# Products with zeros ahead of two output steps of a state space model, and pooling groups in reverse order on GpSimd

## The chip, the core and the metric

The kernel runs on one core of a Trainium2 chip. A core has five engines, each with its own queue of instructions, which it works off in order: TensorE (PE: matrix products, and PEld, its weight loads), VectorE (DVE), ScalarE (ACT), GpSimd (POOL) and SyncE (SP), which issues most of the DMAs. Engines wait for each other by semaphores. The metric is the device time of one execution in microseconds (us).

## The reference

Two transformer stacks over one sequence of 256 tokens of 1024 channels, in fp32. The first has two layers: a gated delta rule mixer with a SwiGLU feed-forward layer, then a state space mixer (S5) with a mixture of eight experts, of which each token uses two. The second stack has one layer: a mixer and an MLP. The change touches the S5 mixer and the second stack's mixer. What they compute, cut to what matters:

```python
def s5_mixer(x, w_in, lam_re, lam_im, log_dt, b_re, b_im, c_re, c_im, d_skip, w_glu):
    u = (x @ w_in).astype(f32)
    ...
    def step(h, u_c):
        bu = jnp.einsum('gpc,btgc->btgp', b_bar, u_c.astype(jnp.complex64))
        _, hs = lax.associative_scan(binop, (jnp.broadcast_to(a_bar, bu.shape), bu), axis=1)
        hs = hs + a_pow[None] * h[:, None]
        y = jnp.einsum('gcp,btgp->btgc', c, hs).real
        return hs[:, -1], y
    ...
    hid = jax.nn.gelu(y.astype(x.dtype), approximate=False)
    val, gate = jnp.split(hid @ w_glu, 2, axis=-1)
    return val * jax.nn.sigmoid(gate)

def pool_mixer(u, w_pool, pool_scale):
    # four groups of 128 channels, windows 2, 4, 8, 16
    ...
        outs.append(mean - u32[:, :, sl])
    mixed = jnp.einsum('btgc,gcd->btgd', pooled, w_pool)
    return mixed.reshape(B, T, POOL_WIDTH) * pool_scale
```

Beside `pool_mixer`, the second stack's mixer has attention of 8 heads over a 64-column grid of tokens: scores, softmax with a mask, and the product with v.

## The kernel before

Everything runs on one core, one stage after the other, in the order of the reference. Matrix products of fp32 are split: each operand has an upper part (`wh`, `hid[0]`) and a remainder (`wl`, `hid[1]`), and the helper `mm3` issues three products per tile, lines 354, 355 and 356: upper by upper, remainder of the weights by upper, upper by remainder. It keeps the product that it issued last in `self.mm`. Weights come by DMA into `wr` (three buffers); ACT makes `wh` of it (line 308) and DVE, seldom POOL, `wl` (line 310), with five buffers each.

Work beside the main stream is written as generators, which `spawn` puts on a list with a lag; `tick` lets them go on between the products of the main stream. The order on each engine is fixed when the program is built, by a scheduler that knows what each instruction depends on. `tc.issue_after(inst)` makes what is issued inside come behind `inst` in that order; it adds no data.

The helper `warm(n)` (lines 272 to 279) issues n bf16 products of a zero tile of 128 x 64 with 512 zero columns into a PSUM bank of its own that nobody reads. Before the change it is called at four places, with the counts of the table `WARM` (line 45).

**S5** works on eight blocks k of 8 groups of channels. For each k, `maps` builds the matrices of the recurrence (products pbt and pk), `states` turns u (pt), makes the inputs of the states (px), scans on DVE (line 1327) and writes the states at the chunk starts into CC (DVE, line 1337), and `outputs(k)` does the following: eight small products pyi of CC with C (line 1349), a copy Y (ACT, line 1350), products yp of u with a band matrix (line 1358) and of Y with the identity (line 1360), the update of uT (DVE, line 1362), Gelu into h (ACT, line 1364), and the split into hid (ACT line 348, DVE line 349). Twelve products `po` of hid with w_glu per block, lines 354 to 356, follow as soon as hid(k) is there; we call them po(k). While the first blocks run, the last products pu of u = x @ w_in are still being issued. The rest of the w_glu products come behind po(7), one dense stream.

**The second mixer** issues products pqk for q and k (lines 354 to 356), for each pair of heads j the scores (line 1929, psc), the bias (DVE, line 1932), the maximum (lines 1936, 1937), Exp on ACT with the row sums in z (line 1939), the reciprocal of z on DVE (line 1940), and the scaling Pr on POOL (line 1942). z has two buffers. At the same time `pool(g)` runs for the four groups g: g+1 additions w on POOL (line 1976, each with the doubled step of the one before), the product with the reciprocal counts, d (line 1984), the difference d - u (line 1985), and then one product ppl with w_pool (line 1988), a copy m1 on ACT (line 1990) and m2 on DVE (line 1991). pool(g) is spawned in the order g = 0, 1, 2, 3 with the lags 3 to 6.

Of the kernel before, what the change touches and what calls it, by code (L numbers as in the profile page):

```python
# [23 lines left out]
KT = D // 128  # L24
# [17 lines left out]
LAG = dict(nb=6, d=5, dp=4, n=1, rk=3, ks=4, kp=4, inv=7, i0=3, iy=8, i1=2, i2=1, lv=4, rq=4, qs=8, qp=2, v=2)  # L42
S5L = dict(per=4, s0=3, t0=9, m=1, o=0, mb=2, a=2, b=2, c=2, d=4, e=2, f=1, g=1, ct=4, gt=4, keep=2)
MO = dict(d=3, t=2, b=5, a=2, sc=1)
WARM = dict(a=12, b=9, c=20, e=5, f=0)
PACE = (1200, 650)
MAGIC = 12582912.0
CH = 4
NJ = T // CH
# [155 lines left out]
class Kern:  # L205
# [66 lines left out]
    def warm(self, n):  # L272

        if not n:
            return
        pb = self.bank("warm")[:64].rearrange("p (a b) -> p a b", a=8)
        for _ in range(n):
            self.nc.tensor.matmul(pb, lhsT=self.zero, rhs=self.zero[:, None, :].to_broadcast([128, 8, 64]), start=True,
                                  stop=True)


# [111 lines left out]
    def load_first(self):  # L393
# [8 lines left out]
        nc.vector.memset(self.zero, 0.0)  # L402
        self.warm(WARM["a"])
        nc.sync.dma_start(xT[:, 0:4, :], a["xT"][:, 0:1024])
# [842 lines left out]
    def s5(self, tables):  # L1247
        nc, tc, a = self.nc, self.tc, self.a
# [6 lines left out]
        MM, TR = nc.tensor.matmul, nc.tensor.transpose  # L1255
# [84 lines left out]
        def outputs(k):  # L1340

            while k not in known:
                yield 1
            C = B[:, k].rearrange("p g c n -> p (g c n)").rearrange("p (g o c) -> p g (o c)", g=8, o=CH)
            H = CC[:, 8 * k:8 * k + 8, :]
            Y = P2.tile([NJ, CH, 8, 16], F32, tag="Y", name="Y")
            py = self.bank("pyi").rearrange("p (g f) -> p g f", g=8)
            for g in range(8):
                MM(py[:NJ, g, :], lhsT=H[:, g, :], rhs=C[:, g, :], start=True, stop=True)
            nc.scalar.activation(Y.rearrange("j o g c -> j g o c"), py[:NJ].rearrange("p g (o c) -> p g o c", o=CH), AF.Copy)  # L1350
            yield S5L["g"]
            while not hid:
                yield 1
            BD = bds.pop(k)
            yp = self.bank("yp")[:, :T].rearrange("p (o j) -> p o j", o=CH)
            for n in range(CH):
                o = min(n, CH - 2)
                MM(yp[:, o:, :], lhsT=BD[:, n, :], rhs=uT[:, k, 1 + o - n:CH + 1 - n, :], start=n == 0, stop=False)
            for o in range(CH):
                MM(yp[:, o, :], lhsT=Y[:, o].rearrange("j g c -> j (g c)"), rhs=ident[:NJ, :NJ], start=False, stop=o == CH - 1)  # L1360
            y = uT[:, k, 1:, :]
            STT(y, y, self.small("sd", k), yp, op0=ALU.mult, op1=ALU.add)
            h = P2.tile([128, T], F32, tag="h", name="h")
            nc.scalar.activation(h.rearrange("p (j o) -> p o j", o=CH), y, AF.Gelu)
            self.split(hid[0][:, k, :], hid[1][:, k, :], h)
            known.add(("hid", k))
# [17 lines left out]
        def flow():  # L1384
            for s in range(12 * KT):
                due = []
                for f, at in ((outputs, S5L["s0"] + S5L["o"] + S5L["a"] + S5L["b"] + S5L["c"] + S5L["d"]), (states, S5L["s0"]),
                              (maps, S5L["s0"] + S5L["m"])):
                    k, r = divmod(s - at, S5L["per"])
                    if 0 <= k < KT and not r and (k > 1 or f != maps):  # L1390
                        self.spawn(f(k))
                yield 1
# [25 lines left out]
        def done(t, n, po):  # L1418
# [18 lines left out]
            else:  # L1437
                self.warm(WARM["e"])
                for _ in logits(t, n):
# [10 lines left out]
        def logits(t, n):  # L1450

            if n == 0:
                xf[t] = (tables, P)[t].tile([128, KT, 128], F32, tag=("CX", "CY")[t], name="xf")
            if (t, n) == (0, 0):
                pl.append(self.bank("pl"))
            nc.scalar.activation(xf[t][:, 2 * n:2 * n + 2, :], self.turn4(self.rr[:, t, n * 256:n * 256 + 256], 2), AF.Copy)
            yield 1
            for kt in range(2 * n, 2 * n + 2):
                MM(pl[0][32 * t:32 * t + 8, :128], lhsT=self.wr[:, kt, :], rhs=xf[t][:, kt, :], start=kt == 0, stop=kt == KT - 1)

        def routed(t):
# [8 lines left out]
            if t:  # L1470
                with tc.issue_after(turned.ins):
                    self.warm(WARM["b"])
            self.ln_apply(t, self.route(t, pb) if t else None)
# [63 lines left out]
    def moe(self):  # L1537
# [13 lines left out]
        def select(es):  # L1551
            m = es.stop - es.start
            for t in range(2):
                r = TT(Sel[:, t, es], iota[:, None, :].to_broadcast([128, m, 128]),
                       pos[:, t, es].unsqueeze(2).to_broadcast([128, m, 128]), op=ALU.is_equal)
            return r
        chosen = select(slice(0, 2))
        self.warm(WARM["f"])

# [159 lines left out]
        with tc.issue_after(self.mm.ins):  # L1719
            self.warm(WARM["c"])  # L1720
        xn = P.tile([128, 2, D], F32, tag="SelT", name="xn")
# [177 lines left out]
    def mixer(self):  # L1899
        nc, tc, a = self.nc, self.tc, self.a  # L1900
# [5 lines left out]
        MM, TR = nc.tensor.matmul, nc.tensor.transpose  # L1906
# [8 lines left out]
        k = P.tile([128, 4, T], F32, name="k")  # L1915
# [51 lines left out]
        def pool(g):  # L1967

            e = slice(8, 8 + T)
            prev = u[:, g, :]  # L1970
            for i in range(g + 1):
                w = P2.tile([128, T + 16], F32, tag="w", name="w")
                lo, hi = (1, 0) if i == 0 else (2 ** (i - 1), 2 ** (i - 1))
                n = T + 16 - lo - hi if i < g else T
                o = lo if i < g else 8
                PT_(w[:, o:o + n], prev[:, o - lo:o - lo + n], prev[:, o + hi:o + hi + n], op=ALU.add)  # L1976
                if i < g:

                    nc.gpsimd.memset(w[:, 0:o], 0.0)
                    if hi:  # L1980
                        nc.gpsimd.memset(w[:, o + n:], 0.0)
                prev = w
            d = P2.tile([128, T], F32, tag="d", name="d")
            PT_(d, prev[:, e], c2[:, g, :], op=ALU.mult)
            PT_(d, d, u[:, g, e], op=ALU.subtract)
            yield 4
            pb = self.bank("ppl")[:, :T]
            MM(pb, lhsT=wpool[:, g, :], rhs=d, start=True, stop=True)
            sc = self.small("pscale", g)
            nc.scalar.activation(self.m1[:, g, :], pb, AF.Copy, scale=sc)  # L1990
            STT(self.m2[:, g, :], pb, sc, self.m1[:, g, :], op0=ALU.mult, op1=ALU.subtract)
# [12 lines left out]
        pb = self.bank("prr")[:, :T]  # L2004
# [3 lines left out]
        for t in range(2):  # L2008
            self.spawn(first(t, self.pbs[t]))
        for g in range(4):  # L2010
            self.spawn(pool(g), 3 + g)
        for j in range(4):
            for dst in (q, k):
                pb = self.bank("pqk", True)[:, :T]
# [41 lines left out]
```

## Time and profile before

| | us |
|---|---|
| median of 3 runs | 1281.87 (1281.63 to 1282.15) |
| the profiled execution | 1283.42 |
| its span, first to last instruction | 1281.6 |
| PE busy | 1232.8 (96%) |
| DVE busy | 1025.7 (80%) |
| ACT busy | 738.4 (58%) |
| POOL busy | 152.6 (12%) |

The granted TensorE clock has a mean of 0.981 of full speed. The profile comes from one execution, and its times are microseconds from the span's first instruction. A timeline gives an instruction's start, its duration, its engine, line and operation, what it writes and reads, and how many stand in the row; in brackets how long the engine was idle before it, and who ended that. The duration of products that follow each other overlaps with the next one's, so the distance of two starts is what one takes up. The eight small fp32 products of a pyi show as x16.

### The profile page before, as it was taken

How to read it: one execution, taken by the hardware profiler on the slowest of the kernel's cores; microseconds unless marked ns; L12 is line 12 of the kernel's file. 1: busy time of each engine (PE TensorE's matmuls, PEld its weight loads, DVE VectorE, ACT ScalarE, POOL GpSimd, SP SyncE). 2: the span in 40 equal slices, each digit the busy share in tenths (PEclk: the TensorE clock that was granted, in tenths of full speed). 3: DMA queues.
4: the chain of work that ended last, by engine and by line, in shares of the span. 5: the costliest groups of instructions: out<-in, count | busy, mean ns of one | idle time of the engine just before them, and what ended most of it. 6: DMA issues, size and time to landing. Idle time of an engine off the chain costs nothing. (4 is left out here: it accounts for less than half of the span.)

```text
span 1281.6 us, 19707 instructions
## 1 busy us (share of the span) xinstructions
PE 1232.8 (96%) x7579; PEld 1064.4 (83%) x7579; DVE 1025.7 (80%) x1565; ACT 738.4 (58%) x1111; POOL 152.6 (12%) x154
## 2 busy tenths in 40 slices
PE   8999999999998899989999999999999999999997
PEld 7998987999986787758888888888877677999886
DVE  6678878989987788678998999999879785766453
ACT  5744455564433553458777776767767465655442
POOL 2323000000102266110000000000002090000000
PEclk8999999999998999989999999999999899999999
DMA  8344225545794300337998989989977543545551
GB/s 330 128 144 141 88 79 203 179 165 197 209 245 187 131 34 34 132 123 281 359 347 303 352 328 362 339 318 379 341 286 298 197 173 132 198 171 192 193 185 50
DMA packets 45589, 273.37 MB, mean 213 GB/s; under 512 B 9008, under 2 KB 9408, under 8 KB 18096
## 3 DMA queue, kind: packets, MB, share of 16 engines
q1 hardware_dynamic: 40320, 257.12, 54.9%
q10 hardware_dynamic: 4336, 10.19, 2.2%
q0 software_dynamic: 832, 4.73, 1.6%
q8 instruction: 62, 1.02, 0.3%
q14 instruction: 39, 0.32, 0.1%
HBM read 266.51 MB, written 1.31 MB: 209 GB/s over the span
## 5 line engine op out<-in xcount | busy, mean ns | idle before, releaser
L310 DVE TENSOR_TENSOR wl<-wr,wh 128x1024 fp32r<-128x1024 f32 (+1 forms) x380 | 447.5, 1195 | 130.8 <-ACT wh L308 127.8
L308 ACT ACTIVATE wh<-wr 128x1024 fp32r<-128x1024 f32 (+2 forms) x390 | 390.9, 1025 | 241.4 <-PE po L356 79.4
L356 PE MATMUL pup<-wh,xg 128*128 128x512 f32 (+1 forms) x384 | 145.1, 378 | 3.0 <-PEq L1680 3.0
L355 PE MATMUL pup<-wl,xg 128*128 128x512 f32 (+1 forms) x384 | 146.3, 381 | 0.1
L354 PE MATMUL pup<-wh,xg 128*128 128x512 f32 (+1 forms) x384 | 146.3, 381 | 0.0
L310 DVE TENSOR_TENSOR wl<-wx,wh 128x1024 fp32r<-128x1024 f32 (+2 forms) x111 | 124.2, 1152 | 11.2 <-ACT wh L308 9.1
L308 ACT ACTIVATE wh<-wx 128x1024 fp32r<-128x1024 f32 (+1 forms) x112 | 105.0, 981 | 9.9 <-PE pup L356 5.9
L354 PE MATMUL p<-x,wh 128*128 128x256 f32 x320 | 90.7, 284 | 0.3 <-ACT s L1013 0.3
L356 PE MATMUL p<-x,wl 128*128 128x256 f32 x320 | 90.6, 283 | 0.0
L355 PE MATMUL p<-x,wh 128*128 128x256 f32 x320 | 90.5, 283 | 0.0
L356 PEld LDWEIGHTS pup<-wh,xg 128*128 128x128 f32 x384 | 72.6, 189 | 14.3 <-issue 3.4
L355 PEld LDWEIGHTS pup<-wl,xg 128*128 128x128 f32 x384 | 72.7, 189 | 13.8 <-DVE wl L310 3.5
L354 PEld LDWEIGHTS pup<-wh,xg 128*128 128x128 f32 x384 | 72.7, 189 | 10.9 <-issue 0.2
L355 PE MATMUL pdn<-wl,eh 128*128 128x512 f32 x176 | 70.0, 398 | 0.8 <-DVE wl L310 0.8
L354 PE MATMUL pdn<-wh,eh 128*128 128x512 f32 x176 | 69.9, 397 | 0.0
L356 PE MATMUL pdn<-wh,eh 128*128 128x512 f32 x176 | 69.5, 395 | 0.0
L354 PE MATMUL pm<-x,wh 128*128 128x256 f32 x224 | 63.5, 283 | 0.0
L356 PE MATMUL pm<-x,wl 128*128 128x256 f32 x224 | 63.4, 283 | 0.0
L355 PE MATMUL pm<-x,wh 128*128 128x256 f32 x224 | 63.4, 283 | 0.0
L354 PEld LDWEIGHTS p<-x,wh 128*128 128x128 f32 x320 | 61.4, 192 | 0.6 <-ACT s L1013 0.5
L355 PEld LDWEIGHTS p<-x,wh 128*128 128x128 f32 x320 | 61.4, 192 | 0.1
L356 PEld LDWEIGHTS p<-x,wl 128*128 128x128 f32 x320 | 61.4, 192 | 0.0
(515 smaller groups left out, 2931.8 us busy)
## 6 DMA issues: line engine op xcount, KB each, us to landing
wr<-w_e SPq DMA_DIRECT2D x59, 1024.0 KB, 6.1
wx<-w_e SPq DMA_DIRECT2D x37, 1024.0 KB, 6.5
wr<-w_f SPq DMA_DIRECT2D x33, 1024.0 KB, 4.8
wr<-w_e SPq DMA_DIRECT2D x29, 768.0 KB, 5.1
wr<-w_up SPq DMA_DIRECT2D x16, 1024.0 KB, 4.6
wr<-w_dn SPq DMA_DIRECT2D x16, 1024.0 KB, 4.6
wx<-w_e SPq DMA_DIRECT2D x19, 768.0 KB, 4.6
wr<-w_glu SPq DMA_DIRECT2D x8, 1024.0 KB, 4.5
```

Source lines behind the costliest of these rows:

```text
L308: self.hi = nc.scalar.activation(hi[:, :w], src, AF.Copy)
L310: self.los[self.n_split] = eng.tensor_tensor(lo[:, :w], src, hi[:, :w], op=ALU.subtract)
L354: mm(out, lhsT=l1, rhs=r1, start=start, stop=False)
L355: mm(out, lhsT=l1, rhs=r2, start=False, stop=False)
L356: self.mm = mm(out, lhsT=l2, rhs=r1, start=False, stop=stop)
```

## The change

Two counts join the table `WARM`: g = 14 and h = 11. `warm` now keeps its last product in `self.idle`. In `outputs(k)`, for k = 0 (g) and k = 7 (h), the zero products are issued behind `self.mm`, the product that `mm3` issued last up to there, and the eight pyi products are issued behind the last zero product. In the mixer `pool(3 - g)` takes the place of `pool(g)`. No value that the kernel writes changes. From line 1349 on, lines of the changed kernel stand 6 further down.

```diff
-WARM = dict(a=12, b=9, c=20, e=5, f=0)
+WARM = dict(a=12, b=9, c=20, e=5, f=0, g=14, h=11)
...
-            self.nc.tensor.matmul(pb, lhsT=self.zero, rhs=self.zero[:, None, :].to_broadcast([128, 8, 64]), start=True,
+            self.idle = self.nc.tensor.matmul(pb, lhsT=self.zero, rhs=self.zero[:, None, :].to_broadcast([128, 8, 64]), start=True,
                                   stop=True)
...
+
+            idle = WARM.get({0: "g", KT - 1: "h"}.get(k))
+            if idle:
+                with tc.issue_after(self.mm.ins):
+                    self.warm(idle)
             py = self.bank("pyi").rearrange("p (g f) -> p g f", g=8)
-            for g in range(8):
-                MM(py[:NJ, g, :], lhsT=H[:, g, :], rhs=C[:, g, :], start=True, stop=True)
+            with tc.issue_after(self.idle.ins) if idle else nullcontext():
+                for g in range(8):
+                    MM(py[:NJ, g, :], lhsT=H[:, g, :], rhs=C[:, g, :], start=True, stop=True)
...
         for g in range(4):
-            self.spawn(pool(g), 3 + g)
+            self.spawn(pool(3 - g), 3 + g)
```

PE's queue around outputs(7), from the last product of po(5) on. Before:

```order
L356 MATMUL po<-wh,hid 128x512
L1349 MATMUL pyi<-B,CC 64x64 x8
L1358 MATMUL yp<-uT,BDs 128x256
L354 MATMUL po<-wh,hid 128x512
L355 MATMUL po<-wl,hid 128x512
L354 MATMUL po<-wh,hid 128x512
L355 MATMUL po<-wl,hid 128x512
L1358 MATMUL yp<-uT,BDs 128x192
L356 MATMUL po<-wh,hid 128x512 x2
L1358 MATMUL yp<-uT,BDs 128x128 x2
L1360 MATMUL yp<-cg,Y 128x64 x4
```

And with the change; of the eleven pairs of a zero weight load and a zero product, one is shown:

```order
L356 MATMUL po<-wh,hid 128x512
L354 MATMUL po<-wh,hid 128x512
L355 MATMUL po<-wl,hid 128x512
...
L356 MATMUL po<-wh,hid 128x512
L278 LDWEIGHTS zero
L278 MATMUL warm<-zero 64x512
...
L1355 MATMUL pyi<-B,CC 64x64 x8
L356 MATMUL po<-wh,hid 128x512
L1364 MATMUL yp<-uT,BDs 128x256
L1364 MATMUL yp<-uT,BDs 128x192
L1364 MATMUL yp<-uT,BDs 128x128 x2
L1366 MATMUL yp<-cg,Y 128x64 x4
L356 MATMUL po<-wh,hid 128x512
```

Seven products of po(6) (three pairs of lines 354 and 355, then one of 356) now stand ahead of the zeros and of pyi(7). Behind yp(7) four more of po(6) follow, and then po(7).

ACT's queue at the same place, from the Y of outputs(7) on. Before:

```order
L1350 ACTIVATE Y<-pyi 64x8x4x16
L1364 ACTIVATE h<-uT 128x4x64
L348 ACTIVATE hid<-h 128x256
L839 DMA gb<-lnrow 128x2048
L1424 ACT_TABLE_LOAD
```

With the change:

```order
L1356 ACTIVATE Y<-pyi 64x8x4x16
L1370 ACTIVATE h<-uT 128x4x64
L308 ACTIVATE wh<-wr 128x1024
L348 ACTIVATE hid<-h 128x256
L839 DMA gb<-lnrow 128x2048
```

One weight cast moved from behind the table load to between h(7) and hid(7); on DVE its wl moved with it, ahead of the lower half of hid(7). It waits for the last product of po(6).

POOL's queue in the mixer, from the addition of group 3 that stands last ahead of the first Pr, to the last d. Before:

```order
L1976 TENSOR_TENSOR w<-u 128x271
L1979 MEMSET w 128x1
L1942 ISA
L1942 TENSOR_SCALAR Pr<-Pr,z 128x256 x6
L1984 TENSOR_TENSOR d<-w,c_14954 128x256
L1985 TENSOR_TENSOR d<-d,u 128x256
L1976 TENSOR_TENSOR w<-w 128x270
...
L1942 TENSOR_SCALAR Pr<-Pr,z 128x256
L1976 TENSOR_TENSOR w<-w 128x268
...
L1942 TENSOR_SCALAR Pr<-Pr,z 128x256
L1976 TENSOR_TENSOR w<-w 128x256
L1984 TENSOR_TENSOR d<-w,c_14954 128x256
L1985 TENSOR_TENSOR d<-d,u 128x256
```

With the change, from the last addition, that of group 0:

```order
L1982 TENSOR_TENSOR w<-u 128x256
L1948 ISA
L1948 TENSOR_SCALAR Pr<-Pr,z 128x256 x6
L1990 TENSOR_TENSOR d<-w,c_14981 128x256
L1991 TENSOR_TENSOR d<-d,u 128x256
L1948 TENSOR_SCALAR Pr<-Pr,z 128x256 x2
L1990 TENSOR_TENSOR d<-w,c_14981 128x256
L1991 TENSOR_TENSOR d<-d,u 128x256
```

All ten additions now stand ahead of the first Pr, seven did before; the last d stands behind eight Pr in both.

## Rows read from the trace of the kernel before

**Rows 1.** Timeline of PE, place 1: start, duration, operation, count, idle before
```profile
438.48 0.46 PE L1305 MATMUL pt<-cg,S 64*128 64x64 f32 x4
...
443.71 1.94 PE L1349 MATMUL pyi<-B,CC 128*64 128x64 f32 x16 [3.62 <-issue]
...
455.75 1.15 PE L1349 MATMUL pyi<-B,CC 128*64 128x64 f32 x16
```

**Rows 2.** Timeline of PE, place 2, from po(5) to po(7)
```profile
518.66 0.40 PE L355 MATMUL po<-wl,hid 128*128 128x512 f32 x1
518.89 0.39 PE L356 MATMUL po<-wh,hid 128*128 128x512 f32 x1
522.15 1.94 PE L1349 MATMUL pyi<-B,CC 128*64 128x64 f32 x16 [2.87 <-DVE CC L1337]
...
527.40 1.10 PE L1360 MATMUL yp<-cg,Y 64*128 64x64 f32 x8
...
530.21 0.50 PE L354 MATMUL po<-wh,hid 128*128 128x512 f32 x1
```

**Rows 3.** Timeline of PE in the mixer: one score product, the last pool product
```profile
1042.23 0.70 PE L1929 MATMUL psc<-k,q 64*128 64x256 f32 x4
...
1052.49 0.70 PE L1988 MATMUL ppl<-d,wpool 128*128 128x256 f32 x2 [1.06 <-POOL d L1985]
```

**Rows 4.** Windows: length, busy time of each engine, granted PE clock, DMA share, GB/s
```profile
443.00:454.00 11.00, 10.29 (x58) 9.46 (x59) 10.75 (x10) 4.17 (x7) 7.84 (x6) 0.53 0.21 84
521.00:526.00 5.00, 3.85 (x22) 3.46 (x23) 2.56 (x4) 2.41 (x4) 0.00 (x0) 0.66 0.00 2
573.00:574.00 1.00, 1.00 (x7) 1.00 (x6) 1.00 (x3) 1.00 (x2) 1.00 (x1) 0.51 0.00 0
```

**Rows 5.** Timeline of DVE, place 1
```profile
442.82 0.68 DVE L1337 TENSOR_TENSOR CC<-p,q 128x504 f32<-128x504 f32 x1
...
462.96 0.48 DVE L1362 SCALAR_TENSOR_TENSOR uT<-uT,sm,yp 128x256 f32<-128x256 f32 x1 [0.32 <-PE yp L1360]
...
465.63 0.69 DVE L1323 TENSOR_TENSOR q<-X,SS 64x512 f32<-64x512 f32 x1 [0.60 <-ACT X L1317]
```

**Rows 6.** Timeline of PE in the routing stage: zero products, and an idle time
```profile
566.12 3.82 PE L278 MATMUL warm<-zero 128*64 128x512 bf16 x9
...
572.23 2.24 PE L1613 MATMUL pxg<-Sel,xt 128*128 128x256 f32 x12 [1.11 <-ACT xt L1500]
```

**Rows 7.** Timeline of ACT, place 2: wh, hid(6), hid(7)
```profile
521.91 1.05 ACT L308 ACTIVATE wh<-wr 128x1024 fp32r<-128x1024 f32 x1
522.87 0.40 ACT L348 ACTIVATE hid<-h 128x256 fp32r<-128x256 f32 x1
...
529.74 0.42 ACT L348 ACTIVATE hid<-h 128x256 fp32r<-128x256 f32 x1
```

**Rows 8.** Timeline of DVE, place 2: the lower half of hid(6)
```profile
524.14 0.41 DVE L349 TENSOR_TENSOR hid<-h,hid 128x256 fp32r<-128x256 f32 x1
```

**Rows 9.** Timeline of POOL in the mixer
```profile
1036.81 7.15 POOL L1942 TENSOR_SCALAR Pr<-Pr,z 128x256 f32<-128x256 f32 x6
...
1045.46 0.64 POOL L1976 TENSOR_TENSOR w<-w 128x270 f32<-128x270 f32 x1
...
1049.51 1.30 POOL L1976 TENSOR_TENSOR w<-w 128x256 f32<-128x256 f32 x1
...
1051.71 0.73 POOL L1985 TENSOR_TENSOR d<-d,u 128x256 f32<-128x256 f32 x1
```

**Rows 10.** Timeline of ACT in the mixer: the third Exp
```profile
1038.68 0.51 ACT L1939 ACTIVATE Pr<-s,m 128x256 f32<-128x256 f32 x1 [0.32 <-POOL Pr L1942]
```

**Rows 11.** Timeline of DVE in the mixer: k of the third pair of heads
```profile
1039.96 0.40 DVE L2019 TENSOR_TENSOR k<-pqk,rows 128x256 f32<-128x256 f32 x1
```

## The prediction

> **What bounds the kernel now.** I read first the waits of TensorE (PE) around the three places that the diff touches. In the state space model PE waits long twice, both times before the products pyi of line 1349: 3.62 us ahead of those of block 0 [rows 1] and 2.87 us ahead of those of block 7 [rows 2]. In the last block's mixer it waits once, 1.06 us, before the last pool product ppl, for POOL's difference d [rows 3]. Elsewhere in the two last places PE is fed, so a microsecond of PE there is a microsecond of the end.
>
> Next the windows. From 443 to 454 us the granted clock averages 0.53, nearly all at the lower of TensorE's two levels (1.2 and 2.4 GHz), and DVE is busy for 10.75 of the 11 us; from 521 to 526 the clock's mean is 0.66 [rows 4]. Both stretches follow the two waits. Then the timelines. In the first place the eight pyi products take 1.94 us, against 1.15 one block later [rows 1]. What they wait for is a DVE row: CC starts at 442.82, lasts 0.68 and ends at 443.50; pyi starts at 443.71. (The profile names no releaser and calls this wait "issue", but it opens with that row.) DVE itself is first kept waiting by PE at 462.96, for 0.32 us [rows 5]. So **place 1 is DVE's**: PE's slow products lie beside DVE's rows and are nearly hidden by them.
>
> In place 2, PE ends po of block 5 at 519.28, waits 2.87 us for CC of block 7, and has line 1360, the end of yp(7), done at 528.50; po(7) starts at 530.21 [rows 2]. That start hangs on yp, uT (DVE), h and hid (ACT), 1.7 us from 528.50. Behind it PE is dense, so here **PE's path is the end's**: whatever delays yp(7) or hid(7) comes out whole.
>
> **The change, part by part.**
>
> *Place 1: fourteen zero products* between pt (ends 438.94 [rows 1]) and pyi(0); eight pu products that ran there move behind pyi. Products of 512 columns follow each other every 0.23 us at the full clock (518.66 to 518.89 [rows 2]), so the zeros end near 442.2. PE then still waits 1.5 us for the same CC, whose time does not move, because DVE's rows ahead of it hang on nothing that the change touches. If the clock stays up, pyi saves 0.79 us and the eleven microseconds together at most 11 x (1 - 0.53) = 5.2 us, of which the eight pu (256 columns, so 0.12 each) take 1.0 back. The end sees only what DVE gets of this: its wait of 0.32, hence -0.3 at best. If the clock falls all the same in the 1.5 us, the eight pu end up to 8 x 0.21 = 1.7 us later (0.21 is half a zero product at the lower clock, nine of which take 3.82 [rows 6]); ACT casts the next weights wh behind them and DVE makes wl from that, so the block loop starts up to 1.7 later. Both ends are open: an idle of 1.11 us at 572 [rows 6] was followed by 0.51 at 573 to 574 [rows 4]. I take **-0.2**: the row it is nearest to is DVE's 0.32, since fourteen products are a denser cover than what stood ahead of that idle.
>
> Here a rule speaks for more. The Trainium skill, "TensorE: Matmul & The Clock Gate", section "Why this matters for your kernels", wants no long idle gaps between bursts of products, since the clock drops after them. By it the whole 5.2 us would be PE's to gain; the trace agrees that the clock is low behind 3.62 and 2.87 us of idle.
>
> *Place 2: eleven zero products.* They are issued behind the mm3 product recorded last, and the order above shows which that is: one of po(6). PE now meets seven products of po(6), the zeros, pyi(7), one more po, yp(7), and then the rest. But po(6) needs hid(6), which ACT writes from 522.87 to 523.27 [rows 7], later than the CC that pyi(7) waited for. So PE's wait grows from 2.87 to 4.0 us (519.28 to 523.3), **the zeros stand behind the gap and not in it**, and the clock falls as before. Step by step:
> - Seven po products from 523.3. The lower half of hid(6) is there at 524.55 [rows 8], in time for the seventh. Before, the five microseconds from 521 lost 5 x 0.34 = 1.7 us, that is the clock was low for some 3 us from pyi on; so all seven run at half, 0.43 each (twice 0.215): 526.3.
> - Eleven zeros at 0.23: 528.8.
> - From pyi(7) to the end of yp(7) took 6.35 us before (522.15 to 528.50 [rows 2]). Now pyi is 0.79 shorter and five po products fewer lie between, three of them at half then (3 x 0.43 + 2 x 0.23 = 1.75): 3.8 us, so 532.6, **+4.1**.
> - On ACT a weight cast wh now stands between h(7) and hid(7). It waits for the last po(6) product, four behind line 1360 (0.9 us), which is there before h(7) is, as hid(7) could start 1.24 behind line 1360 [rows 2, 7]. So wh costs its own step, 0.96 us (521.91 to the 522.87 of the next row [rows 7]).
>
> po(7) starts near 535.3 instead of 530.21: **+5.0**. Bounds: +3.6, if the clock is never low here (the seven products then end at 524.9, as soon as hid's lower half allows); +7.1, if it comes back only behind the zeros (11 x 0.19 more).
>
> *Mixer: longest group first.* POOL's work ahead of the last d stays the same in sum: the same adds, d rows and eight Pr. So that d still ends near 1052.44 [rows 9]; the wait before ppl can go only where POOL saves something elsewhere: -1.06 at best. Against it, three adds that stood among the Pr rows (two of 0.64 and one of 1.30 us) stand before the first one now: it comes 2.6 us later than 1036.81 [rows 9]. ACT's Exp at 1038.68 waits for that Pr, whose buffer of sums z it takes over [rows 10]; behind Exp DVE's queue has the reciprocal of z and then k at 1039.96 [rows 11]. All move by about 2.5. The score product that reads this k starts at 1042.23 [rows 3], 1.87 us after k's end at 1040.36, so it comes 0.6 late, and the next score products, which wait for DVE rows still further behind in that queue, up to 2.5. Part of it falls into the 1.06 us that PE waited for d anyway. Bounds -1.06 and +2.5; I take **+1.3**, the 2.5 less what falls into that wait, as the rows of the delay are all measured and those of a gain are not.
>
> Sum: -0.2 + 5.0 + 1.3 = **+6.1 us**. The profiled execution took 1283.42 us, span 1281.6, which is 1.55 above the median of the three runs; the sum is a difference and is put on the median: 1281.87 + 6.1 = **1288.0 us**. With the bounds (-0.3 + 3.6 - 0.3 to -0.2 + 7.1 + 2.3) the forecast's own range is 1284.8 to 1291.
>
> **Rivals.**
> - *PE paces place 1*, the page's rule carried through. If DVE's rows there end when they do because of PE after all, the whole 5.2 us comes; with the wait for d gone (-1.06) and place 2 at its cheapest (+3.6) that is -2.7: **1279.2**, faster. It decides if the first q row of block 3 on DVE comes at 461 us or earlier, not at 465.63 [rows 5]. For it: the clock row. Against it: DVE busy for 10.75 of 11 us. Chance 0.12.
> - *The parts cancel*: half of the 5.2 comes through (-2.6), place 2 costs +3.6 and the mixer -0.3, that is +0.7: **1282.6**. For it: vector rows stretch with what runs beside them (on POOL an add of 256 columns took 1.30 us where one of 270 took 0.64 [rows 9]), so an earlier PE may shorten some of DVE's. Against: as above. Chance 0.16.
> - *The clock falls once more.* Place 1 at +1.7; in place 2 PE now idles about 1.8 us before po(7) instead of 0.1, and if that costs a stretch like 521 to 526, another 1.7: +1.7 + 6.7 + 1.3 = +9.7, **1291.6**. For it: the fall behind 1.11 us of idle. Against: dense products on both sides. Chance 0.12.
> - The forecast, the zeros of place 2 behind the gap: 0.60.
>
> **How the numbers follow.** A measurement of this kernel tells 0.2% (2.6 us) from no change. Faster by more: the first rival, 0.12. Within: the second, and a few hundredths of the forecast where all its bounds are low: 0.18. Slower: 0.70. The range leaves out one in ten at either end: from 1279.5, which leaves out most of the first rival, to 1291.0, which leaves out most of the third.
>
> **What would show it.** Right: PE waiting about 4 us before po(6) and none before pyi(7); a clock near half from 523 on; wh between h(7) and hid(7); po(7) 5 us later, counted from the first q row of block 3. In place 1 a clock of 1.0 from 444 to 454, CC at its old time and that q row within 0.5 us of 465.6. In the mixer the first Pr near 1039.4 (shifted by what went before) and PE waiting for k or s, not for d. Wrong: no wait before po(6), or po(7) less than 3 us later; the q row 3 us early; or the last ppl earlier, counted from the mixer's start.

## The result, and the profile after

The changed kernel takes 1294.46 us (median of 6 runs, 1291.03 to 1295.21), against 1281.86 for the kernel before (6 runs, 1281.35 to 1285.73). The medians lie 12.6 us apart; the ratio of the two sets of runs is put at 1.0079 (95%: 1.006 to 1.0098), which makes it slower by 10.1 us (7.7 to 12.6). The prediction had the sign, but not the size: 1288.0, with a range from 1279.5 to 1291.0.

The profiled execution took 1295.07 us, its span is 1293.3, 11.7 more than before. Busy times, from the page of the changed kernel:

```profile
PE 1240.1 (96%) x7604; PEld 1067.3 (83%) x7604; DVE 1027.8 (79%) x1565; ACT 738.7 (57%) x1111; POOL 153.2 (12%) x154
```

PE is busy for 7.3 us more; its two rows of zeros alone are 6.95 (3.21 and 3.74, below). To find where it arose, take rows that both traces have and compare the distance from one to the next:

| stretch, from row to row | before | after | more |
|---|---|---|---|
| start to the CC ahead of pyi(0) (code unchanged) | 442.82 | 443.48 | +0.66 |
| place 1: to the first q of block 3 on DVE | 22.81 | 24.47 | **+1.66** |
| block loop: to the end of po(5) | 53.65 | 53.71 | +0.06 |
| place 2: to the start of po(7) | 10.93 | 17.23 | **+6.30** |
| routing and experts: to the last u of the mixer (unchanged) | 494.51 | 495.17 | +0.66 |
| mixer: to the copy v on ACT | 32.49 | 35.19 | **+2.70** |
| rest: to the end | 224.39 | 224.05 | -0.34 |

The three places make 10.3 of the 11.7 together with the small gain at the end. The two unchanged stretches are not the change's: in the profiles below, the start alone lies between 1.0 shorter and 3.2 longer.

**Place 2.** The timeline of PE in the changed kernel, from the gap to po(7) (it answers to [rows 2]):

```profile
525.69 0.80 PE L354 MATMUL po<-wh,hid 128*128 128x512 f32 x1 [4.03 <-ACT hid L348]
...
528.42 0.63 PE L356 MATMUL po<-wh,hid 128*128 128x512 f32 x1
528.98 3.74 PE L278 MATMUL warm<-zero 128*64 128x512 bf16 x11
532.55 1.09 PE L1355 MATMUL pyi<-B,CC 128*64 128x64 f32 x16
...
535.21 1.10 PE L1366 MATMUL yp<-cg,Y 64*128 64x64 f32 x8
...
538.89 0.50 PE L354 MATMUL po<-wh,hid 128*128 128x512 f32 x1 [1.45 <-ACT hid L348]
```

The gap has grown from 2.87 to 4.03 us, it ends with hid(6), and the zeros stand behind it. The timeline of ACT at hid(7) (to [rows 7]):

```profile
536.86 0.66 ACT L1370 ACTIVATE h<-uT 128x256 f32<-128x256 f32 x1 [2.58 <-DVE uT L1368]
537.47 1.06 ACT L308 ACTIVATE wh<-wr 128x1024 fp32r<-128x1024 f32 x1
...
538.43 0.40 ACT L348 ACTIVATE hid<-h 128x256 fp32r<-128x256 f32 x1
```

The windows of the changed kernel at both places (to [rows 4]; length, busy times, then granted clock):

```profile
443.00:454.00 11.00, 9.55 (x80) 8.62 (x80) 10.69 (x11) 4.18 (x8) 7.38 (x6) 1.00 0.27 97
462.00:470.00 8.00, 8.00 (x42) 6.34 (x41) 4.06 (x5) 3.37 (x6) 3.79 (x3) 0.57 0.00 0
524.00:531.00 7.00, 5.31 (x12) 3.04 (x13) 1.95 (x3) 1.64 (x3) 0.00 (x0) 0.54 0.00 1
531.00:532.00 1.00, 1.00 (x5) 0.49 (x4) 0.00 (x0) 0.00 (x0) 0.00 (x0) 0.80 0.00 0
532.00:533.00 1.00, 1.00 (x12) 0.71 (x11) 0.00 (x0) 0.00 (x0) 0.00 (x0) 1.00 0.00 0
```

The seven po products and about half of the zeros ran at the lower level; the full one was back near 531.4.

**Place 1.** The first window shows what the zeros were put there for: 1.00 from 443 to 454, where it was 0.53. Yet DVE is busy for 10.69 of the 11 us, as before, and the next rows come no earlier. The second window shows a fall that the kernel before doesn't have. Its own window there:

```profile
462.00:470.00 8.00, 8.00 (x66) 6.61 (x66) 5.79 (x8) 4.92 (x9) 3.32 (x3) 1.00 0.01 2
```

The timeline of PE of the changed kernel at both (to [rows 1]):

```profile
439.55 3.21 PE L278 MATMUL warm<-zero 128*64 128x512 bf16 x14
444.37 1.12 PE L1355 MATMUL pyi<-B,CC 128*64 128x64 f32 x16 [1.61 <-issue]
...
455.98 2.13 PE L1279 MATMUL pk<-CX,B 128*128 128x128 f32 x8 [0.78 <-DVE uT L1368]
...
461.50 0.73 PE L356 MATMUL po<-wh,hid 128*128 128x512 f32 x2 [1.48 <-DVE hid L349]
...
465.20 1.97 PE L1315 MATMUL px<-U,BT 64*128 64x64 f32 x16
```

And that of DVE (to [rows 5]):

```profile
463.73 0.48 DVE L1368 SCALAR_TENSOR_TENSOR uT<-uT,sm,yp 128x256 f32<-128x256 f32 x1 [0.61 <-PE yp L1366]
...
467.95 0.69 DVE L1323 TENSOR_TENSOR q<-X,SS 64x512 f32<-64x512 f32 x1 [2.14 <-ACT X L1317]
```

PE, now ahead of DVE's rows, waits 0.78 and 1.48 us, the second time for the lower half of hid(0), and the clock falls some 1.6 us later. uT comes 20.25 us behind the CC of this stretch, against 20.14 before: no later. Only then does the time go: the three po products ahead of px are slow (0.7 more), px takes 1.97 instead of 1.11, and DVE waits 2.14 instead of 0.60 us for X, which ACT makes of px. **The slow stretch moved from a place that DVE hides to one that it doesn't.**

**Mixer.** The waits of PE in it, whole:

```profile
PE psc L1935 <- DVE k L2025: 1.4, 1, 1.4
PE psc L1935 <- DVE s L1938: 0.7, 1, 0.7
```

The wait for d [rows 3] is gone and two others are there. Where they come from stands in POOL's timeline (two of its additions, then the first six Pr)

```profile
1037.81 1.60 POOL L1982 TENSOR_TENSOR w<-w 128x256 f32<-128x256 f32 x1
...
1047.84 1.47 POOL L1982 TENSOR_TENSOR w<-u 128x256 f32<-128x256 f32 x1
1049.39 6.25 POOL L1948 TENSOR_SCALAR Pr<-Pr,z 128x256 f32<-128x256 f32 x6
```

and in ACT's: the third Exp, which waited 0.32 us before [rows 10].

```profile
1051.26 0.51 ACT L1945 ACTIVATE Pr<-s,m 128x256 f32<-128x256 f32 x1 [3.84 <-POOL Pr L1948]
```

Counted from the last u (1034.06; 1024.72 before) the first Pr [rows 9] and the third Exp are both 3.24 us later than before. Little of that is made up: at the last of the eight pairs of Exp it is 2.70, and the copy v starts right behind that pair, in both kernels.

### The profile page after: what moved, and what is told of

Same layout as the page of the kernel before. It is cut to its first block, busy times and chain, and to the rows that moved or that the text cites. A ratio compares the mean times of both kernels' runs of the same rounds, so it can differ in the third digit from the quotient of the medians.

```text
span 1293.3 us, 19756 instructions
## 1 busy us (share of the span) xinstructions
PE 1240.1 (96%) x7604; PEld 1067.3 (83%) x7604; DVE 1027.8 (79%) x1565; ACT 738.7 (57%) x1111; POOL 153.2 (12%) x154
```

## The experiments

Each kernel was run on the same chip as runs of the kernel before. Executions of one and the same kernel there spread over 7 to 8 us (25 to 31 runs of before in each of three batches, medians 1283.5 to 1285.0), so ratios settle little below 2 us, and the verdicts go by the distances of the table above, in the one profile of each run. In code that isn't changed these repeat within 0.4 us at place 1 and 0.2 at place 2. The unchanged mixer has two forms: PE waits 1.06 for d, and from the last u to v it takes as long as before (0.0 and 0.0 more in two profiles); or it waits 0.9 for s and 0.26 for d, and takes 0.7 more (four profiles). What goes with the second form is the DMA of the reciprocal counts c, for which POOL's first d waits 0.99 to 1.75 us there and 0.28 to 0.78 in the three profiles of the first form, the kernel before included. In the second form the third Exp then waits 2.17 us for Pr, against 0.32. The first d in the kernel before, then the same row and the third Exp in the run with g alone:

```profile
1026.94 1.40 POOL L1984 TENSOR_TENSOR d<-w,c 128x256 f32<-128x256 f32 x1 [0.28 <-DMA c<-c]
```

```profile
1029.94 1.07 POOL L1990 TENSOR_TENSOR d<-w,c 128x256 f32<-128x256 f32 x1 [1.75 <-DMA c<-c]
```

```profile
1041.27 0.51 ACT L1945 ACTIVATE Pr<-s,m 128x256 f32<-128x256 f32 x1 [2.17 <-POOL Pr L1948]
```

| run | ratio (95%) | place 1 | loop | place 2 | mixer |
|---|---|---|---|---|---|
| reversed groups alone | 1.0011 (0.9996 to 1.0026) | 0.0 | 0.0 | 0.0 | +2.74 |
| g = 14 alone | 1.0013 (1.0 to 1.0026) | +1.58 | +0.1 | +0.2 | +0.7 |
| h = 11 alone | 1.0044 (1.0031 to 1.0057) | -0.3 | 0.0 | +5.29 | 0.0 |
| h, order alone | 1.0029 (1.0018 to 1.004) | -0.4 | 0.0 | +3.59 | +0.7 |
| g = 4 | 1.0025 (1.0013 to 1.0037) | +2.72 | +0.1 | +0.2 | +0.7 |
| g = 14, po(0) behind | 1.0024 (1.001 to 1.0039) | -1.06 | +1.99 | +1.76 | 0.0 |
| six zeros in the gap | 1.0009 (0.9998 to 1.0021) | 0.0 | 0.0 | -0.5 | +0.7 |
| groups 0, 1, 3, 2 | 1.0012 (0.9997 to 1.0027) | +0.1 | 0.0 | +0.1 | +1.43 |
| reversed, four z | 0.9998 (0.9982 to 1.0015) | 0.0 | 0.0 | 0.0 | -0.25 |
| four z | 1.0002 (0.9986 to 1.0017) | 0.0 | 0.0 | 0.0 | +1.53 |
| six zeros, reversed, four z | 0.9995 (0.9979 to 1.0012) | +0.1 | 0.0 | -0.4 | +0.05 |

**Each part alone.** Reversed groups, g and h, each put on the kernel before (g and h with the code that issues the zeros, as in the change).

```diff
-            self.spawn(pool(g), 3 + g)
+            self.spawn(pool(3 - g), 3 + g)
```

> The kernel before, with only the pool groups in reverse order. Theory A (ten additions stand ahead of the first Pr, so Exp, the reciprocal of z, k and the scores come late): the wait before the last ppl is gone, PE waits for k and for s in the mixer instead, and the kernel is about 2.4 us slower than before, near 1284.3. Rival B (the mixer's delay in the changed kernel came from what went before it, not from the order): the kernel is within 0.5 us of before or up to 1 us faster, as the 1.06 us wait goes.

```diff
-WARM = dict(a=12, b=9, c=20, e=5, f=0)
+WARM = dict(a=12, b=9, c=20, e=5, f=0, g=14, h=0)
```

> The kernel before, with only the fourteen zero products and the pyi order of block 0. Theory A (the clock stays up at first, but the end of yp(1) now stands behind six products of po(0), two of which wait for hid(0); PE idles some 2 us, the clock falls later and the block loop starts late): clock 1.0 from 444 to 454, near 0.5 from about 463 to 469, first q of block 3 on DVE 1.7 us later than in the kernel before counted from CC of block 0; about 1.7 us slower, 1283.6. Rival B (that late fall is an accident of the one profiled run): the loop starts within 0.4 us of before and the time is within 0.5 us of 1281.9.

```diff
-WARM = dict(a=12, b=9, c=20, e=5, f=0)
+WARM = dict(a=12, b=9, c=20, e=5, f=0, g=0, h=11)
```

> The kernel before, with only the eleven zero products and the pyi order of block 7. Theory A (the zeros stand behind po(6), which waits for hid(6)): PE waits 4.0 us before po(6), and po(7) starts 6.3 us later than before, counted from the end of po(5); 1288.2. Rival B (half of that came from the clock's state as the changed place 1 left it): +4 or less, 1286 or less.

Each part costs in its own place about what it costs in the whole: +2.74 of 2.70, +1.58 of 1.66, +5.29 of 6.30. The reversed groups and g came as their theories A had it. The three ratios add to 0.68%, the whole has 0.79%. The +6.3 that was expected of h alone did not come: the missing 1.0 is the moment at which the clock falls. Alone, the first products behind the gap still ran at the full level, and it was low from about 525.9 to 529.3.

The run with h alone, in which block 0 is as before, also says something on place 1. There the lower level lasted some 6.8 us and not 10.2, so that PE was early without any zeros. The windows of the kernel before and of h alone:

```profile
443.00:456.00 13.00, 12.29 (x76) 11.16 (x77) 12.72 (x12) 4.71 (x9) 8.22 (x6) 0.61 0.18 71
```

```profile
443.00:456.00 13.00, 10.40 (x81) 9.55 (x82) 12.68 (x13) 4.93 (x9) 7.94 (x6) 0.74 0.23 82
```

PE waited 0.82 for uT and 0.68 for the lower half of hid(0), the clock stayed up behind that, DVE's wait of 0.32 for yp(1) was gone, and q of block 3 came 0.34 earlier (0.36 in the next run, with the same clock). An early PE alone thus gave what the prediction allowed; it takes something else to make a loss of it.

**Place 2: order or zeros.** The order of h is kept, the zeros are not issued:

```diff
-                with tc.issue_after(self.mm.ins):
-                    self.warm(idle)
+                self.idle = self.mm
```

> As the kernel with the place of block 7 alone, but with no zero products: the eight pyi products of block 7 are only issued behind the mm3 product recorded last. Theory A (order and zeros each cost): without the zeros' 3.6 us, and with wh still between h(7) and hid(7), po(7) is 2.7 us later than before, 1284.6. Rival B (the order costs nothing by itself, only the zeros do): within 0.5 us of before, 1281.9. Rival C (the zeros bring the clock back, so that without them the rest runs at half): 4 us later or more, 1286.

Measured +3.59, with the same wait and the same slow products. The timeline of PE of this run:

```profile
524.83 0.80 PE L354 MATMUL po<-wh,hid 128*128 128x512 f32 x1 [4.01 <-ACT hid L348]
...
528.12 1.97 PE L1354 MATMUL pyi<-B,CC 128*64 128x64 f32 x16
530.01 0.52 PE L356 MATMUL po<-wh,hid 128*128 128x512 f32 x1
```

So the order costs 3.6 and the zeros add 1.7 to 2.7. The order costs more than the 2.7 of theory A, as pyi(7) runs slowly too, and rival B is out. In these three profiles the zeros don't bring the clock back sooner: without them the full level is back near 530.0, against 529.3 and 531.4 with them.

**Zeros inside the gap.** Six zeros behind po(5): `mm3` keeps its product before last too, and the zeros are issued behind that one.

```diff
+        self.pm = getattr(self, "mm", None)
...
-                with tc.issue_after(self.mm.ins):
+                with tc.issue_after(self.pm.ins):
```

> Block 7 alone, six zero products, issued behind the last product of po(5) and not behind po(6). Theory A (zeros help where they stand inside the wait): PE waits 1.5 us before pyi(7) in place of 2.9 and some 0.6 us more for hid(6), the clock stays at 1.0 from 519 to 530, and po(7) starts 0.5 to 1.5 us earlier than before, counted from the end of po(5); 1281 against 1281.9 on a quiet chip. Rival B (the clock falls all the same in the remaining idle time): po(7) 0 to 1 us later than before.

The timeline of PE of this run:

```profile
519.10 1.48 PE L278 MATMUL warm<-zero 128*64 128x512 bf16 x6
522.08 0.65 PE L1356 MATMUL pyi<-B,CC 128*64 128x64 f32 x8 [1.50 <-DVE CC L1338]
523.24 0.50 PE L354 MATMUL po<-wh,hid 128*128 128x512 f32 x1 [0.51 <-ACT hid L348]
```

The products are at full speed from here to po(7), which starts 0.5 us earlier than before. The last run below repeats it. So with zeros inside the gap the clock stayed up, twice, and what they gain is small; it can't be told from no change in the total.

**Place 1: clock or order.** First only four zeros, in the same order:

```diff
-WARM = dict(a=12, b=9, c=20, e=5, f=0, g=14, h=0)
+WARM = dict(a=12, b=9, c=20, e=5, f=0, g=4, h=0)
```

> Block 0 alone, with four zero products in place of fourteen; every other product stands in the same order as with fourteen. Theory A (the order does no harm; what costs is where the low stretch of the clock lies): PE idles 3.8 us before pyi(0), the clock is low from about 443 to 454, where DVE sets the pace, and high from 462 on; the first q of block 3 comes within 0.4 us of the kernel before, counted from the start of pt(S). Rival B (the end of yp(1) behind six po products costs by itself): that q is 1.5 us late again, or more.

Measured +2.72. The first stretch is slow up to 449 (clock 0.52 from 442 to 449), the wait for hid(0) is there, and so is the second fall (0.54 from 464 to 470). DVE's and PE's rows of this run:

```profile
450.31 1.43 DVE L310 TENSOR_TENSOR wl<-wr,wh 128x1024 fp32r<-128x1024 f32 x1 [1.46 <-ACT wh L308]
```

```profile
461.01 0.73 PE L356 MATMUL po<-wh,hid 128*128 128x512 f32 x2 [1.47 <-DVE hid L349]
```

The low stretch was as long as with h alone, and the zeros few; what differs is the order, and with it +2.72 stands against -0.34. So the order brings the loss. The fourteen zeros take 1.1 of it back, and the first row shows how: without them the pu products behind pyi(0) are slow, wh comes late, DVE waits 1.46 for it, and uT of block 1 comes 1.14 later than with fourteen. Then the fourteen zeros, with po(0) started only when hid(1) is there, so that only one of its products stands ahead of the end of yp(1):

```diff
-            while ("hid", k) not in known:
+            while ("hid", max(k, 1)) not in known:
```

> Block 0 alone with its fourteen zeros, but the products po(0) are issued only when hid(1) is, so that the end of yp(1) stands behind one po product and not behind six. Theory A (the wait for hid(0) inside yp(1) opened the idle time after which the clock fell): no wait for hid inside yp(1), uT(1) a little earlier, the clock stays at 1.0 up to 470, and the first q of block 3 is within 0.4 us of before or up to 0.4 earlier. Rival B (the clock falls there whatever the order, because PE is idle for want of work): near 0.5 in some five microseconds between 458 and 470, and q late by 1 us or more.

The timeline of PE of this run at yp(1):

```profile
455.03 2.13 PE L1279 MATMUL pk<-CX,B 128*128 128x128 f32 x8 [0.76 <-DVE uT L1368]
458.53 1.10 PE L1366 MATMUL yp<-cg,Y 64*128 64x64 f32 x8
460.55 0.50 PE L356 MATMUL po<-wh,hid 128*128 128x512 f32 x1 [0.49 <-DVE hid L349]
460.98 1.11 PE L1315 MATMUL px<-U,BT 64*128 64x64 f32 x16
```

The wait of 1.48 is 0.49 and stands behind yp(1), the clock stays at 1.00 from 441 to 464, and q of block 3 comes 1.06 earlier than in the kernel before. That is more than the 0.3 that the prediction allowed and the 0.4 expected of this run: DVE's wait for yp(1) is gone, and so is its wait of 0.60 for X [rows 5]. But it is given back: in the block loop PE then waits four times for S on ACT (3.8 us in all), the loop is 1.99 longer, the gap before pyi(7) is 4.3, and two products of po(5) are left over behind it. Counted from the CC ahead of pyi(0), the router's first product pl, behind both places, comes 2.5 later than before.

**Mixer: how many additions ahead.** The groups 0, 1, 3, 2: eight additions ahead of the first Pr instead of seven or ten.

```diff
-            self.spawn(pool(g), 3 + g)
+            self.spawn(pool((0, 1, 3, 2)[g]), 3 + g)
```

> The kernel before with the pool groups in the order 0, 1, 3, 2: eight additions stand ahead of the first Pr (seven before, ten in reverse order), the last d again behind eight Pr. Theory A (the delay of the first Pr reaches PE only past the slack of the scores, 1.9 us): the first Pr is 0.7 to 0.9 us late, PE does not wait for k, the 1.1 us wait before the last ppl stays, and the stage is within 0.4 us of before. Rival B (any delay of the first Pr comes out whole): 0.7 to 0.9 us slower.

The first Pr is 0.86 late, the third Exp waits 2.08 for Pr and is 1.87 late, PE waits 0.83 for s and not for d, and v is 1.43 late, 0.7 more than in the slower of the two unchanged forms. Both expectations were lower. It points to the delay of Pr coming out, but in one profile, beside forms 0.7 apart, it doesn't settle it. The next does.

**Mixer: take the wait away.** Four buffers for z, so that Exp need not wait for Pr. The instructions on every engine stay in the order of the reversed groups alone.

```diff
-                z = P2.tile([128, 2], F32, tag="z", name="z")
+                z = P2.tile([128, 2], F32, tag="z", name="z", bufs=4)
```

> The kernel before with the pooling groups in reverse order and four buffers for z instead of two; the order on every engine is that of the run with the reversed groups alone, only Exp need not wait for Pr any more. Theory (the late first Pr costs through Exp's wait for z's buffer, then the reciprocal, k and psc): Exp of the third pair starts right behind the weight cast, k is not late, PE waits neither for k nor for s; the last ppl hangs on d again. From the last u to v then about -0.4 to +0.4 us against before (the run with the reversed groups alone: +2.7). Rival A (the delay is in POOL itself, which the mix step and ppl wait for): still +1.5 or more, with PE waiting for d or Pr. Rival B (the adds ahead slow DVE and ACT rows beside them): k late by 1 us or more without any wait of Exp.

The timeline of ACT in this run, with the third Exp (the last u starts at 1024.16):

```profile
1037.42 0.50 ACT L1939 ACTIVATE Pr<-s,m 128x256 f32<-128x256 f32 x1
```

Its timeline of POOL, with the first six Pr:

```profile
1039.50 6.16 POOL L1942 TENSOR_SCALAR Pr<-Pr,z 128x256 f32<-128x256 f32 x6
```

And that of PE, with the last pool product:

```profile
1051.68 0.70 PE L1988 MATMUL ppl<-d,wpool 128*128 128x256 f32 x2 [0.94 <-POOL d L1985]
```

The first Pr is as late as with the reversed groups and two buffers, 15.34 us behind the last u (12.09 in the kernel before), and it costs nothing: Exp no longer waits, k is on time, PE waits for d alone, and the 2.74 us have become -0.25 (+0.05 in the last run below). So the loss of the mixer went through z's two buffers, which is shown; what the order of the groups is worth beside that is less than the two unchanged forms differ by. The same four buffers in the old order:

> The kernel before with four buffers for z, groups in the old order, the same order on every engine. Theory: Exp's wait of 0.32 us for Pr goes, nothing of it reaches the end, as the last ppl waits for d: 0.0 from the last u to the last ppl (unchanged code gave 0 to 0.75), PE still waits about 1 us for d. Rival: the wait mattered, then -0.3 us or more and a d that comes earlier.

The wait for d was 1.53 here instead of 1.06, the last ppl came 0.35 late, and v 1.53. POOL's first d waited 1.09 for c, as in the slower form. The windows of this run behind that wait:

```profile
1055.01:1056.01 1.00, 1.00 (x6) 0.60 (x6) 0.00 (x0) 0.26 (x1) 1.00 (x2) 1.00 0.00 0
...
1057.01:1058.01 1.00, 1.00 (x3) 0.74 (x3) 0.99 (x3) 0.69 (x3) 1.00 (x2) 0.50 0.00 0
```

The clock fell to the lower level some 1.4 us behind that wait, which accounts for 1.18 of the 1.53 (the stretch from the last ppl to v). So this run neither shows a gain nor rules one out below that.

**Both remedies together.** Six zeros in the gap, reversed groups, four z, no g.

> Six zeros inside the wait of place 2 (as in the run with six early zeros), none at place 1, the reversed groups with four buffers for z. Theory: place 2 -0.5, mixer -0.4 to +0.4, so 0 to -1 us in all, which the runs cannot tell from none: ratio 0.998 to 1.001. Rival: the reversed groups cost for another reason than z's buffers, then +1 to +2 us in the mixer.

Ratio 0.9995 (0.9979 to 1.0012), mixer +0.05, and place 2 takes 0.4 us less than before, with the clock at 1.00 through it. No version beats the kernel before by an amount that these runs can tell.

## Why the prediction was wrong in size

| term | predicted (bounds) | measured |
|---|---|---|
| place 1 | -0.2 (-0.3 to +1.7) | +1.66, alone +1.58 |
| place 2 | +5.0 (+3.6 to +7.1) | +6.30, alone +5.29 |
| mixer | +1.3 (-1.06 to +2.5) | +2.70, alone +2.74; 0.3 to 0.4 given back behind v |
| sum | +6.1 | +10.3 |

**Place 1: the step "The end sees only what DVE gets of this: its wait of 0.32, hence -0.3 at best" failed.** For the eleven microseconds behind the zeros it was right: clock 1.00, DVE the pace, uT on time, and where PE was early in the old order (h alone) the 0.3 came. It did not follow PE on to the next wait. There the new order moved the last product of uT and the first of Y of yp(1) behind two po products that wait for the lower half of hid(0), as the rest of yp(1) did before. The wait was 1.48 us with the new order (1.47 with four zeros), 0.68 with an early PE in the old order, and none in the kernel before. Behind 1.48 the clock fell, behind 0.68 it didn't, and the slow products lay on the way to px, on which DVE's next row hangs; that is the +1.66. The step also left out DVE's wait of 0.60 for X, which stands in its own rows [rows 5], so -0.3 was not the best that the place can give (-1.06 with po(0) behind). The upper bound of +1.7 had the right size by chance, from another mechanism: a fall right behind pyi, slow pu products, a late wh. That one shows with four zeros, as 1.14 on top.

The Trainium skill, "TensorE: Matmul & The Clock Gate", section "Why this matters for your kernels", wants gaps between bursts kept short; this trace agrees on the clock (0.53 to 1.00), and not on the time, as PE was not what set it there. The first rival, which carried that rule through, is refuted: q of block 3 had to come at 461 and came at 467.95.

**Place 2: the mechanism is shown, and the term "Eleven zeros at 0.23" was mis-sized.** By its own steps, in us:

| step | predicted | measured |
|---|---|---|
| gap before po(6) | 4.0 | 4.03 |
| seven po products | 3.0 | 3.29 |
| eleven zeros | 2.5 | 3.57 |
| pyi(7) to the end of yp(7) | 3.8 | 3.8 |
| from there to po(7), with wh in it | 2.7 | 2.6 |

The clock was low for some 3.4 us before, from pyi(7) on, and the prediction let it be low for 3.0. It stayed low for 6.8 us, from ahead of the first po product on (3.4 in the run with h alone, 6.8 in that without zeros), so about half of the zeros ran at half speed. Why it lasts 3.4 in one run and 6.8 in another, behind the same wait of 4.0, stays open. The prediction's bound "only behind the zeros" covers both.

**Mixer: the step "the 2.5 less what falls into that wait" failed.** The late Pr, the wait of Exp, the late k and s and the end of the wait for d are all there as named. Two sizes were off. The first Pr came 3.24 late and not 2.6, as the additions ahead of it took longer than those they were priced by (the last one 1.47). And nothing was to be deducted. PE's 1.06 of waiting for d stood beside a chain from one Exp to the next, over s, z, k and the score products, and this chain carried the delay to v (3.24 at the third pair, 2.70 at the last), while d lay off it. The run with four z shows it: the same late Pr, no delay. With nothing deducted, the term was +2.5, and +2.70 came.

**The rivals.** "The parts cancel" is out with place 1. "The clock falls once more", 1291.6, came nearest in total, but its second half did not happen: PE idled 1.45 us before po(7), and from po(7) on the next stage ran as before (-0.06, to the last product ahead of the routing's first zeros). That its +1.7 at place 1 fits is the chance named above. The forecast of zeros behind the gap was right, and so was its sign; three terms each short by 1.3 to 1.9 put the time above the range. The range was also drawn too narrow by the prediction's own working: its upper end takes place 1 at -0.2 and the mixer at +2.3, though their own bounds were +1.7 and +2.5. With these the sum reaches 11.3, 1293.2, and the change of 10.1 lies inside.

## What to carry to other kernels

Filler products lost time here where they stood behind the gap, and where DVE set the pace and the order moved with them; inside the gap, with PE setting the pace, they gained at most 0.5 us. So ask what sets the pace in the stretch, read from the order which product the anchor really is, compare the order of everything else, and follow PE to its next wait after the gain. When work is pulled ahead on a slow engine, ask which buffer its late successor holds: here two buffers of two numbers per partition carried the whole delay to ACT, DVE and PE, and two more took it away. A wait that disappears from the list is no gain if another one opened ahead of it.

## What the runs showed of the hardware

- The same idle time was followed by either level. Waits of PE of 0.94 and 1.06 us before the last ppl left the clock at 1.00, one of 1.53 at the same place was followed by 0.50 some 1.4 us later. In place 1, 1.61 us behind fourteen zeros left it at 1.00, and so did 0.76 and 0.49 later on, and 0.82 and 0.68 with h alone; 0.78 and 1.48 there were followed by a fall.
- The fall comes late and lasts: in place 1 the products right behind the wait of 1.48 still ran fast, and the slow ones were those from some 1.6 us later on, with no idle time among them. At place 2 the low stretch lasted some 3.4 us before and with h alone, and 6.8 in the changed kernel and in the run with h's order alone.
- POOL's additions of 256 columns took between 0.61 and 1.60 us in the changed kernel's mixer. What stretches them wasn't tried.
